# Three reorderings in a delta net: norm factors, convolutions, and the queue of four small writes

## The chip, the cores and the metric

The kernel runs on one core of a Trainium2 chip. Its time is the device time of one execution in microseconds (us); of several executions the median is given. The core's engines each work through their own list of instructions in order: TensorE (PE, matmuls), VectorE (DVE), ScalarE (ACT), GpSimd (POOL) and SyncE (SP, which here only issues DMAs). A DMA is issued by one of these engines, as an instruction in that engine's list, and then runs beside it.

## The reference

The program computes two transformer blocks for one sequence of 256 tokens with 1024 features. The change touches the first layer, a gated delta net. Cut to what matters:

```
qkv  = silu(causal_conv(hn @ w_in))        # 4 taps; q, k: 8 heads, v: 16 heads, 128 each
q, k = l2norm(q) * 128**-0.5, l2norm(k)    # the norm needs a sum over each head
m    = strict_lower((k*beta) @ k^T * decay)   # per head and chunk of 64 tokens
t    = inverse(m + I)                      # triangular solve
u, w = t @ (v*beta), t @ (k*beta*exp(gc))
... a recurrence over the chunks uses u, w, q and k
o    = rmsnorm(o) * silu(z)                # z is a fourth part of hn @ w_in
out  = o @ w_out
```

The decay comes from the gates g and beta, which are 32 more columns of `hn @ w_in`.

## The kernel before

All large products are in fp32 at higher precision: a weight chunk of 128 x 1024 is loaded by SP (`wr`, line 172), ACT copies its high part (`wh`, line 186), DVE subtracts that to give the low part (`wl`, line 187), and each product is three matmuls on PE, lines 249 to 251: high by high, high by low, low by high. Chunks have four buffers each for `wr`, `wh` and `wl`, and `_prep` asks for a chunk two chunks ahead of its use. The delta net's projections come in the order keys, gates, then a mix of q, z and v groups (`ORDER = "qqzqqzvvvvvvzvvz"`). Groups of q, k and v have matmuls of 256 columns, z groups of 512. PSUM has eight banks in one pool, `ps`.

Work that is not a projection is written as generators, "sides". `tick()` advances each side once per four weight tiles, so the point in a side's code at which it yields decides beside which projection its instructions are written. A scheduler then takes the program as written, with a priority for each instruction (its place in the program, less an offset inside `tc.high_priority`), and sets the final order on each engine from these priorities and the dependencies. `behind(i, p)` adds a dependency without a semaphore: instruction i may only stand after p in the order.

The sides and helpers that the change touches or that follow from it, all in `gdn_body`:
- `conv` (line 644): for each of two 256-column halves ACT writes tap 3 (`cy`, line 651), DVE adds taps 2, 1 and 0 (line 654), then ACT's Silu reads both halves (line 655). For q and k ACT then squares the result (`sqg`, line 665), and PE sums the squares into the bank `ssb` (line 673) after `WSSB` yields.
- `factors(0)` (line 682): when the sums of the keys are there, DVE computes the norm factors, ACT takes a logarithm (line 694), DVE adds the gates (`bgc`).
- `x_stage` (line 701): behind `factors(0)`, for each of eight head pairs PE writes `kk` = k k^T (lines 707, 708) and for two heads a bank `rp` with the gates' differences (lines 711, 712); ACT takes three exponentials of it into `EA` (lines 713 to 715), DVE multiplies `XA = -kk * EA` (line 716). After pairs 4 and 8 the diagonal 32 x 32 blocks of eight heads go to DRAM in eight small DMAs of 32 KB each (`s<-XA`, line 722). `Q[0]` is SP's queue.
- `inv_stage` (line 745): POOL reads all of that back in another layout (`NT`, line 756). DVE then does 31 steps of a substitution, each of two instructions (`fst`, line 764, and `TI`, line 766), copies the result (`TP`, line 771); SP writes `TP` and `TI` to DRAM and reads them back as blocks of `XA` and of `h`.
- `levels` (after that): 32 x 32 and 64 x 64 matmuls `y1p` (line 832), `z1p` (841, 842), `y2p` (854), `z2p` (857) for four quarters of the heads build the full inverse; between them ACT and DVE copy the results back into `Y`, `h` and `XA` (lines 833, 843, 845, 860).
- `a_stage` (line 729): PE writes `kq`, DVE multiplies it with `EA` (line 740). `evac_v` transposes v (`vtp`, line 795); `evac_z` copies z (`zt`, line 808).

Of the kernel before, what the change touches and what calls it, by code (L numbers as in the profile page):

```python
# [14 lines left out]
ALU = mybir.AluOpType  # L15
# [5 lines left out]
T = 256  # L21
# [96 lines left out]
PRIO = 0  # L118
CY = 2
CZ = 2  # L120
WSSB = 9
WVTP = 6
WINV = 10
ACCN = 4
# [18 lines left out]
class Builder:  # L143
# [31 lines left out]
    def _prep(self, j):  # L175
        if j in self.halves or j >= 2 * NCH:
            return
        nc = self.nc
        for i in range(j, j + 3):
            self._raw(i)  # L180
        r = self.raws.pop(j)
        self.raws[j] = None
        hi = self.wtile(j, F32R, "wh")
        lo = self.wtile(j, F32R, "wl")
        with self.tc.high_priority(offset=PRIO):
            nc.scalar.activation(hi, r, AF.Copy)  # L186
            i = nc.vector.tensor_tensor(lo, r, hi.bitcast(F32), ALU.subtract)  # L187
        if j in self.pins:
            self.behind(i, self.pins[j])
        self.halves[j] = (hi, lo)  # L190

    def behind(self, i, p):
# [37 lines left out]
    def w(self, name, r0, c0, width=P):  # L230
        nt = max(width // P, 1)
        self.ticks += nt
        if self.ticks >= 4:
            self.ticks -= 4
            self.tick()
        if self.n % 8 + nt > 8:
            self.n += 8 - self.n % 8
        j = self.n // 8
        for i in range(j, j + self.LA + 1):
            self._prep(i)  # L240
        self.spec.append((self.n, name, r0, c0, width))
        o = (self.n % 8) * P
        self.n += nt
        hi, lo = self.halves[j]
        return hi[:, o : o + width], lo[:, o : o + width]
# [330 lines left out]
    def gdn_body(self, gp, x):  # L576
        nc, tc, sp = self.nc, self.tc, self.sp
# [3 lines left out]
        blk = lambda b: slice(32 * b, 32 * b + 32)  # L581
# [21 lines left out]
        XA = XAb.rearrange("p k h c -> p h k c")  # L603
# [42 lines left out]
        def conv(bank, ct, dst):  # L646
            y = t2([P, 2, T], "cy")
            for i in range(2):
                u = bank[:, i * T : i * T + T]
                w = lambda j: self.col("aconv", (ct + i) * 4 + j)  # L650
                nc.scalar.activation(y[:, i], u, AF.Copy, scale=w(3))
                for j in (2, 1, 0):
                    n = 3 - j
                    nc.vector.scalar_tensor_tensor(y[:, i, n:], u[:, : T - n], w(j), y[:, i, n:], ALU.mult, ALU.add)  # L654
            nc.scalar.activation(dst, y, AF.Silu)

        kT, qT = big("kT"), big("qT")
# [2 lines left out]
        def mk_evac(dst, off, ct0, key):  # L660
            def evac(g, b):
                d = dst[:, 2 * g : 2 * g + 2]
                conv(b, ct0 + 2 * g, d)
                sq = sp.tile([P, 2, T], F32, tag="sq", bufs=2, name="sqg")
                nc.scalar.activation(sq, d, AF.Square)

                def later():
                    for _ in range(WSSB):
                        yield
                    for i in range(2):  # L670
                        for tt in range(2):
                            c = off + tt * 8 + 2 * g + i
                            nc.tensor.matmul(ssb[:, c : c + 1], sq[:, i, tt * P : tt * P + P], self.ones[:, 0:1], start=True, stop=True)  # L673
                    st[key] += 1

                self.side(later())

            return evac


        def factors(o):
            s = slice(o, o + 16)
            nc.vector.tensor_scalar(var[:, s], ssb[:, s], EPS, None, ALU.add)
            nc.vector.tensor_copy(rk[:, s], self.rsqrt(var[:, s], (P, 16)))
            if o == 0:
                nc.vector.tensor_tensor(irk[:, s], var[:, s], rk[:, s], ALU.mult)
                nc.vector.tensor_tensor(rk2[:, s], rk[:, s], rk[:, s], ALU.mult)
                for tt in range(2):
                    nc.vector.scalar_tensor_tensor(
                        lnc[:, tt * 16 : tt * 16 + 16].rearrange("p (a b) -> p a b", b=2),  # L690
                        bg[:, tt, 0:16].rearrange("p (a b) -> p a b", b=2), 1e-30,
                        rk2[:, tt * 8 : tt * 8 + 8].unsqueeze(2).to_broadcast([P, 8, 2]), ALU.max, ALU.mult)

                nc.scalar.activation(lnc, lnc, AF.Ln)
                nc.vector.tensor_tensor(bgc[:, 0:2], bg[:, 0, 32:80].rearrange("p (a b) -> p a b", b=16)[:, 0:3:2],
                                        lnc[:, 0:16].unsqueeze(1).to_broadcast([P, 2, 16]), ALU.add)
                nc.vector.tensor_tensor(bgc[:, 2], bg[:, 1, 32:48], lnc[:, 16:32], ALU.add)

        Q = [{"s": nc.sync, "a": nc.scalar, "g": nc.gpsimd}[c] for c in QS]

        def x_stage():
            while st["kss"] < 4 or not st["bg"]:
                yield
            factors(0)
            for j in range(8):
                kk = self.bank("kk")
                nc.tensor.matmul(ev3(kk)[:, 0:3:2], kT[:, j, 0:P], kT[:, j], start=True, stop=True)
                nc.tensor.matmul(kk[:, P:T], kT[:, j, P:], kT[:, j, P:], start=True, stop=True)
                for h in (2 * j, 2 * j + 1):
                    rp = self.bank("rp")  # L710
                    nc.tensor.matmul(rp[:, :384], identr[:, h : h + 1].to_broadcast([P, P]), gch, start=True, stop=False)
                    nc.tensor.matmul(rp[:, :384], identb, mask3b, start=False, stop=True)
                    nc.scalar.activation(EA[:, h, 0], rp[:, 0:128], AF.Exp, bias=bgc[:, 0, h : h + 1])
                    nc.scalar.activation(EA[:, h, 2], rp[:, 128:256], AF.Exp, bias=bgc[:, 1, h : h + 1])
                    nc.scalar.activation(EA[:, h, 1], rp[:, 256:384], AF.Exp, bias=bgc[:, 2, h : h + 1])
                    nc.vector.scalar_tensor_tensor(XA[:, h], ev3(kk), -1.0, EA[:, h], ALU.mult, ALU.mult)
                st["X"] = j + 1
                if j % 4 == 3:
                    H = slice(2 * j - 6, 2 * j + 2)
                    for b in range(4):  # L720
                        for tt in range(2):
                            Q[0].dma_start(s1[b, tt, H].rearrange("h s t -> s h t"), XA[blk(b), H, tt, blk(b)])
                if j % 4 != 3:
                    yield
                else:
                    for _ in range(4):
                        yield
# [18 lines left out]
        s1 = self.dp.tile([4, 2, 16, 32, 32], F32, name="s1")  # L746
# [38 lines left out]
        def evac_v(g, b):  # L785
            vt = t2([P, 2, T], "vt")
            conv(b, 16 + 2 * g, vt)

            def later():
                for _ in range(WVTP):  # L790
                    yield
                pt = self.bank("vtp")
                for tt in range(2):
                    for i in range(2):
                        nc.tensor.transpose(pt[:, tt * T + i * P : tt * T + i * P + P], vt[:, i, tt * P : tt * P + P], self.ident)
                for tt in range(2):
                    nc.scalar.activation(vn[:, tt, 2 * g * P : 2 * g * P + T], pt[:, tt * T : tt * T + T], AF.Copy,
                                         scale=irk[:, tt * 8 + g : tt * 8 + g + 1])
                st["v"] += 1

            self.side(later())
# [156 lines left out]
        gv = self.gemm("w_in", x, KD, list(range(16, 32)), evac_v)  # L958
        gz = self.gemm_nat("w_in", x, KD, [4096, 4608, 5120, 5632], 512, evac_z)
        self.side(x_stage())  # L960
        self.side(inv_stage())
        self.side(a_stage())
# [998 lines left out]
```

## Time and profile before

| | before |
|---|---|
| median of 3 runs | 1212.6 us (1211.88 to 1213.06) |
| the profiled execution | 1211.13 us |
| its span in the trace | 1209.3 us |
| mean granted TensorE clock | 0.997 of full speed |
| PE busy | 1185.4 us, 98% of the span |
| DVE busy | 890.1 us, 74% |
| ACT busy | 686.7 us, 57% |

The trace is of one execution. Times in it count from the start of the span. A busy share says how long an engine held an instruction, and for PE the ends of matmuls are modelled and neighbours overlap: the distance from one start to the next is what a matmul costs in a row of matmuls. In a timeline row the brackets give how long the engine stood idle before the row, and the work whose end released it.

### The profile page before, as it was taken

The page shows a single profiled execution, that of the slowest core. Times are in us where ns is not written, and L with a number is a line of the kernel's source. Part 1 is how long each engine was busy: PE and PEld are TensorE (multiplying, and loading weights), DVE is VectorE, ACT ScalarE, POOL GpSimd, SP SyncE. Part 2 cuts the span into 40 slices and gives each one's busy share as a digit, 9 for nine tenths or more (in the row PEclk, how much of TensorE's full clock was granted, in tenths as well). Part 3 has the DMA queues.
Part 4 walks back from the last instruction along what each step waited for, and adds up shares of the span by engine and source line. Part 5 has one row for each costly group of instructions (what it writes and reads, how often), then busy time and mean ns, then how long its engine had stood idle before and what let it go on. Part 6 is the DMA issues. An engine that isn't in the chain of part 4 may idle for free.

```text
span 1209.3 us, 23369 instructions
## 1 busy us (share of the span) xinstructions
PE 1185.4 (98%) x9368; PEld 1122.7 (93%) x9368; DVE 890.1 (74%) x1642; ACT 686.7 (57%) x1166; POOL 20.4 (2%) x47
## 2 busy tenths in 40 slices
PE   6999999999999999999999999999999999999997
PEld 6989988999999999989999999889799999999996
DVE  6968977668877778879977878756656567655555
ACT  4786556556655556556655556754465455444443
POOL 1000000000000001000000000000000000000000
PEclk9999999999999999999999999999999999999999
DMA  6546385454655557434655655363255563555552
GB/s 212 187 134 201 120 223 178 140 165 155 208 187 180 188 178 248 131 102 149 206 185 184 192 183 165 116 201 123 88 174 175 176 241 119 180 185 184 188 181 82
DMA packets 68205, 206.00 MB, mean 170 GB/s; under 512 B 18086, under 2 KB 18230, under 8 KB 67841
## 3 DMA queue, kind: packets, MB, share of 16 engines
q1 hardware_dynamic: 65488, 194.77, 50.3%
q0 software_dynamic: 2608, 9.75, 2.3%
q8 instruction: 73, 1.20, 0.4%
q14 instruction: 36, 0.29, 0.1%
HBM read 199.75 MB, written 4.74 MB: 169 GB/s over the span
## 4 chain that ended last, share of the span: by engine, by line
PE 92%; DVE 5%; ACT 2%; issue 1%; DMA 0%; SPq 0%; DVEq 0%; ACTq 0%
PE pb L249 21%; PE pb L250 20%; PE pb L251 20%; PE acc L249 7%; PE acc L251 7%; PE acc L250 7%; DVE wl L187 1%; PE pt L1163 1%; PE ssb L673 1%; DMA ident<-cst 0%; DVE cy L654 0%; PE kv L1567 0%; ACT wh L186 0%; PE y1p L903 0%; PE csum L366 0%
## 5 line engine op out<-in xcount | busy, mean ns | idle before, releaser
L187 DVE TENSOR_TENSOR wl<-wr,wh 128x1024 fp32r<-128x1024 f32 x362 | 442.0, 1224 | 200.0 <-ACT wh L186 198.6
L186 ACT ACTIVATE wh<-wr 128x1024 fp32r<-128x1024 f32 x362 | 381.7, 1056 | 335.8 <-issue 99.3
L249 PE MATMUL pb<-xh,wh 128*128 128x256 f32 x1224 | 347.7, 284 | 0.6 <-ACT xh L569 0.6
L251 PE MATMUL pb<-xh,wl 128*128 128x256 f32 x1224 | 345.5, 283 | 0.7 <-DVE wl L187 0.7
L250 PE MATMUL pb<-xl,wh 128*128 128x256 f32 x1224 | 345.3, 282 | 0.2 <-DVE xl L570 0.2
L249 PEld LDWEIGHTS pb<-xh,wh 128*128 128x128 f32 x1224 | 231.6, 189 | 2.7 <-issue 1.3
L250 PEld LDWEIGHTS pb<-xl,wh 128*128 128x128 f32 x1224 | 230.3, 188 | 0.5 <-DVE xl L570 0.4
L251 PEld LDWEIGHTS pb<-xh,wl 128*128 128x128 f32 x1224 | 229.5, 188 | 0.9 <-DVE wl L187 0.9
L249 PE MATMUL pb<-fh,wh 128*128 128x256 f32 x416 | 118.4, 285 | 0.0
L250 PE MATMUL pb<-fl,wh 128*128 128x256 f32 x416 | 117.5, 283 | 0.1
L251 PE MATMUL pb<-fh,wl 128*128 128x256 f32 x416 | 116.7, 281 | 0.0
L249 PE MATMUL acc<-ah,wh 128*128 128x256 f32 x352 | 98.7, 280 | 0.0
L251 PE MATMUL acc<-ah,wl 128*128 128x256 f32 x352 | 98.6, 280 | 0.0
L250 PE MATMUL acc<-al,wh 128*128 128x256 f32 x352 | 98.5, 280 | 0.0
L249 PEld LDWEIGHTS pb<-fh,wh 128*128 128x128 f32 x416 | 77.9, 188 | 1.4 <-issue 0.4
L250 PEld LDWEIGHTS pb<-fl,wh 128*128 128x128 f32 x416 | 78.2, 188 | 1.1 <-DVE fl L436 0.3
L251 PEld LDWEIGHTS pb<-fh,wl 128*128 128x128 f32 x416 | 78.9, 190 | 0.0
L1002 DVE SCALAR_TENSOR_TENSOR fy<-fpad,cols,fy 128x256 f32<-128x256 f32 x176 | 73.6, 479 | 0.0
L249 PE MATMUL pb<-wh,xh 128*128 128x512 f32 (+1 forms) x176 | 70.3, 401 | 0.0
L250 PE MATMUL pb<-wl,xh 128*128 128x512 f32 (+1 forms) x176 | 68.2, 388 | 1.1 <-DVE wl L187 1.1
L251 PE MATMUL pb<-wh,xl 128*128 128x512 f32 (+1 forms) x176 | 67.9, 386 | 0.0
L249 PEld LDWEIGHTS acc<-ah,wh 128*128 128x128 f32 x352 | 66.8, 190 | 0.0
(438 smaller groups left out, 2082.7 us busy)
## 6 DMA issues: line engine op xcount, KB each, us to landing
wr<-wall SPq DMA_DIRECT2D x362, 512.0 KB, 3.6
wzd<-zt POOLq DMA_DIRECT2D x8, 256.0 KB, 2.9
wzog<-wzd POOLq DMA_DIRECT2D x4, 512.0 KB, 4.0
bias<-bd POOLq DMA_DIRECT2D x4, 512.0 KB, 7.4
h<-xT SPq DMA_DIRECT2D x4, 256.0 KB, 4.1
h<-xT POOLq DMA_DIRECT2D x1, 1024.0 KB, 7.6
wrow<-wrow POOLq DMA_DIRECT2D x1, 1024.0 KB, 9.0
out_dram<-mw SPq DMA_DIRECT2D x4, 256.0 KB, 2.0
```

The costliest lines, as they stand in the source:

```text
L186: nc.scalar.activation(hi, r, AF.Copy)
L187: i = nc.vector.tensor_tensor(lo, r, hi.bitcast(F32), ALU.subtract)
L249: mm(out, ah, bh, start=start, stop=False, skip_group_check=skip)
L250: mm(out, ah, bl, start=False, stop=False, skip_group_check=skip)
L251: mm(out, al, bh, start=False, stop=stop, skip_group_check=skip)
L673: nc.tensor.matmul(ssb[:, c : c + 1], sq[:, i, tt * P : tt * P + P], self.ones[:, 0:1], start=True, stop=True)
L1002: nc.vector.scalar_tensor_tensor(y[:, i], u[:, i, j : j + T], w(j), y[:, i], ALU.mult, ALU.add)
L1163: nc.tensor.transpose(pt[:, j * P : j * P + P], S[:, i, j * P : j * P + P], self.ident)
```

## The change

Lines in the changed file stand 1 to 6 further down than in the file before: line 187 is the same, 249 to 251 are 250 to 252, 654 is 655, 722 is 728, 833 is 839, 843 is 849. The change has four parts.

- `WSSB` becomes a table with the value 9 for keys and for queries, as before.
- `_prep` remembers the last `wl` instruction written, and the first DVE tap of each convolution's first half may not stand ahead of it.
- `x_stage` writes `factors(0)` with a priority of 60 places earlier, and yields twice before its first head pair.
- Of the last eight small writes, the four with `tt` = 1 are issued by ACT and the other four by SP.

```diff
-WSSB = 9
+WSSB = {"kss": 9, "qss": 9}
...
         if j in self.pins:
             self.behind(i, self.pins[j])
+        self.lastwl = i
         self.halves[j] = (hi, lo)
...
                 for j in (2, 1, 0):
                     n = 3 - j
-                    nc.vector.scalar_tensor_tensor(y[:, i, n:], u[:, : T - n], w(j), y[:, i, n:], ALU.mult, ALU.add)
+                    op = nc.vector.scalar_tensor_tensor(y[:, i, n:], u[:, : T - n], w(j), y[:, i, n:], ALU.mult, ALU.add)
+                    if i == 0 and j == 2:
+                        self.behind(op, self.lastwl)
...
-                    for _ in range(WSSB):
+                    for _ in range(WSSB[key]):
...
-            factors(0)
+            with tc.high_priority(offset=60):
+                factors(0)
+            for _ in range(2):
+                yield
...
-                            Q[0].dma_start(s1[b, tt, H].rearrange("h s t -> s h t"), XA[blk(b), H, tt, blk(b)])
+                            (nc.scalar if j == 7 and tt else Q[0]).dma_start(s1[b, tt, H].rearrange("h s t -> s h t"), XA[blk(b), H, tt, blk(b)])
```

The counts of instructions stay as they were, but for the four DMA issues that go from SP to ACT. The order changes on PE from about 58 us to 217 us of the trace before, and on DVE and ACT beside it.

The first place is ACT's list around the last exponentials of `x_stage` and the first convolution of the queries behind them. The number behind `wr`, `wh` or `wl` tells one chunk's tile from another's. Before:

```order
L715 ACTIVATE EA<-rp,bgc 128x128
L651 ACTIVATE cy<-pb,cols 128x256
L186 ACTIVATE wh_1092<-wr_970 128x1024
L186 ACTIVATE wh_1139<-wr_1060 128x1024
L651 ACTIVATE cy<-pb,cols 128x256
L186 ACTIVATE wh_1163<-wr_1090 128x1024
L651 ACTIVATE cy<-pb,cols 128x256
L655 ACT_TABLE_LOAD
L655 ACTIVATE qT<-cy 128x512
```

And now:

```order
L721 ACTIVATE EA<-rp,bgc 128x128
L186 ACTIVATE wh_1136<-wr_1013 128x1024
L658 ACT_TABLE_LOAD
L658 ACTIVATE qT<-cy 128x512
L728 DMA s_208<-XA 32x8x32
L668 ACTIVATE sqg<-qT 128x512
L728 DMA s_208<-XA 32x8x32 x3
L652 ACTIVATE cy<-pb,cols 128x256
L186 ACTIVATE wh_1157<-wr_1090 128x1024
```

The four issues of line 728 stand behind a `wh` copy, the load of the activation table and the Silu of line 658, and around the Square of line 668; the convolution's `cy` of the same bank is now ahead of the exponentials.

The second place is DVE's list at the end of the inversion. Before:

```order
L766 TENSOR_TENSOR TI<-TI,fst 128x31
L654 SCALAR_TENSOR_TENSOR cy<-pb,cols,cy 128x255
L771 COPY TP<-TI 128x32x32
L654 SCALAR_TENSOR_TENSOR cy<-pb,cols,cy 128x254
L187 TENSOR_TENSOR wl_1820<-wr_1711,wh_1819 128x1024
L654 SCALAR_TENSOR_TENSOR cy<-pb,cols,cy 128x253
L187 TENSOR_TENSOR wl_1845<-wr_1747,wh_1844 128x1024
L654 SCALAR_TENSOR_TENSOR cy<-pb,cols,cy 128x255
L740 SCALAR_TENSOR_TENSOR EA<-kq,EA 128x384
```

And now:

```order
L746 SCALAR_TENSOR_TENSOR EA<-kq,EA 128x384
L655 SCALAR_TENSOR_TENSOR cy<-pb,cols,cy 128x254
L772 TENSOR_TENSOR TI<-TI,fst 128x31
L746 SCALAR_TENSOR_TENSOR EA<-kq,EA 128x384
L655 SCALAR_TENSOR_TENSOR cy<-pb,cols,cy 128x253
L777 COPY TP<-TI 128x32x32
L187 TENSOR_TENSOR wl_1845<-wr_1741,wh_1844 128x1024
L187 TENSOR_TENSOR wl_1863<-wr_1800,wh_1862 128x1024
L746 SCALAR_TENSOR_TENSOR EA<-kq,EA 128x384 x2
L187 TENSOR_TENSOR wl_1893<-wr_1842,wh_1892 128x1024
```

The taps of line 655 that stood among the weights' low parts behind `TP` now stand ahead of `TP`, and two low parts follow it at once. From the first `fst` up to `TP` there are now 37 taps (31 before) and 13 `wl` (12 before) beside the 62 steps of the inversion.

The third place is ACT's list where the levels begin. Before:

```order
L833 ACTIVATE Y_1947<-y1p 32x256
L833 ACTIVATE Y_2030<-y1p 32x256
L651 ACTIVATE cy<-pb,cols 128x256 x2
L843 ACTIVATE h<-z1p 32x2x4x32
L186 ACTIVATE wh_1972<-wr_1890 128x1024
L845 ACTIVATE XA<-z1p 32x2x4x32
L655 ACTIVATE vt<-cy 128x512
L186 ACTIVATE wh_2067<-wr_1920 128x1024
L860 ACTIVATE Y_2101<-y2p 64x512
```

And now:

```order
L186 ACTIVATE wh_1952<-wr_1890 128x1024
L839 ACTIVATE Y_1977<-y1p 32x256
L652 ACTIVATE cy<-pb,cols 128x256 x2
L849 ACTIVATE h<-z1p 32x2x4x32
L186 ACTIVATE wh_2014<-wr_1915 128x1024
L658 ACTIVATE vt<-cy 128x512
L851 ACTIVATE XA<-z1p 32x2x4x32
L839 ACTIVATE Y_2072<-y1p 32x256
L186 ACTIVATE wh_2097<-wr_1950 128x1024
L866 ACTIVATE Y_2131<-y2p 64x512
```

The copy `Y` of the second quarter (`Y_2030` before, `Y_2072` now) stood next to that of the first, and now stands behind two taps, the first quarter's copy into `h`, a `wh`, a Silu and the copy into `XA`. On PE, `y1p` of the first quarter now stands 48 matmuls of 256 columns later in the projections (384 before, 48 more now), and the stretches of about ten projection matmuls ahead of `z1p` and between `z1p` and `y2p` of the first quarter are gone.

## Rows read from the trace of the kernel before

**Rows 1.** The page: busy us (share of span) per engine; chain by engine

```profile
PE 1185.4 (98%) x9368; PEld 1122.7 (93%) x9368; DVE 890.1 (74%) x1642; ACT 686.7 (57%) x1166; POOL 20.4 (2%) x47
...
PE 92%; DVE 5%; ACT 2%; issue 1%; DMA 0%; SPq 0%; DVEq 0%; ACTq 0%
```

**Rows 2.** PE timeline, 60 to 240: start, length, work, [idle before, releaser]

```profile
72.40 0.40 PE L249 MATMUL pb<-wh,xh 128*128 128x512 f32 x1
73.80 0.44 PE L711 MATMUL rp<-gch,identr 128*128 128x384 f32 x1 [1.00 <-ACT EA L715]
...
148.61 0.50 PE L250 MATMUL pb<-wl,xh 128*128 128x512 f32 x1 [1.14 <-DVE wl L187]
...
169.79 0.21 PE L841 MATMUL z1p<-XA,Y 32*32 32x32 f32 x1 [0.46 <-ACT Y L833]
```

**Rows 3.** ACT timeline around the keys' norm factors, same columns

```profile
70.49 1.06 ACT L186 ACTIVATE wh<-wr 128x1024 fp32r<-128x1024 f32 x1 [0.91 <-PE pb L251]
71.57 1.28 ACT L713 ACT_TABLE_LOAD   x1
...
73.38 0.37 ACT L715 ACTIVATE EA<-rp,bgc 128x128 f32<-128x128 f32 x1
```

**Rows 4.** PE timeline: two neighbours of 256 columns, one of 512 between its neighbours

```profile
158.36 0.39 PE L251 MATMUL pb<-wh,xl 128*128 128x512 f32 x1
158.59 0.40 PE L249 MATMUL pb<-wh,xh 128*128 128x512 f32 x1
...
173.24 0.28 PE L250 MATMUL pb<-xl,wh 128*128 128x256 f32 x1
173.36 0.28 PE L251 MATMUL pb<-xh,wl 128*128 128x256 f32 x1
```

**Rows 5.** Second half's small writes: DVE's last product, SP's issues, ACT's Square

```profile
90.82 0.56 DVE L716 SCALAR_TENSOR_TENSOR XA<-kk,EA 128x384 f32<-128x384 f32 x1 [0.22 <-ACT EA L715]
...
91.40 5.39 SPq L722 DMA_DIRECT2D s<-XA  x8
...
99.74 0.61 ACT L665 ACTIVATE sqg<-qT 128x512 f32<-128x512 f32 x1
```

**Rows 6.** All instructions of L722: ns min/median/max, starts; landing times

```profile
L722 SPq DMA_DIRECT2D s<-XA x16: 325/449/2047, 79.8 to 96.3; - x16
...
DMA to landing us min/median/max: 1.5/2.2/3.7
```

**Rows 7.** The read of NT on POOL, and DVE's first step of the inversion

```profile
98.59 0.54 POOL L756 DMA_DIRECT2D NT<-s  x1 [17.50 <-DMA s<-XA]
...
105.62 0.19 DVE L764 TENSOR_TENSOR fst<-NT,TI 128x31 f32<-128x31 f32 x1 [1.89 <-DMA NT<-s]
```

**Rows 8.** DVE timeline behind the inversion's last step

```profile
152.89 1.08 DVE L771 COPY TP<-TI 128x1024 f32<-128x1024 f32 x1
...
155.31 0.47 DVE L654 SCALAR_TENSOR_TENSOR cy<-pb,cols,cy 128x253 f32<-128x253 f32 x1
155.71 1.21 DVE L187 TENSOR_TENSOR wl<-wr,wh 128x1024 fp32r<-128x1024 f32 x1
```

**Rows 9.** Ten microseconds: us, PE, PEld, DVE, ACT, POOL busy, clock, DMA share, GB/s

```profile
140.00:150.00 10.00, 8.86 (x66) 8.14 (x65) 10.00 (x28) 5.75 (x9) 0.00 (x0) 1.00 0.40 111
```

**Rows 10.** DMA issues, 80 to 180: KB each, median us to landing

```profile
XA<-s SPq DMA_DIRECT2D x4, 128.0 KB, 5.2
```

**Rows 11.** PE timeline at the levels

```profile
168.64 0.69 PE L832 MATMUL y1p<-h,XA 32*32 32x32 f32 x30
...
173.93 1.14 PE L854 MATMUL y2p<-h,XA 64*64 64x64 f32 x16
```

**Rows 12.** ACT timeline at the levels

```profile
170.54 0.38 ACT L833 ACTIVATE Y<-y1p 32x256 f32<-32x256 f32 x1 [0.80 <-PE y1p L832]
...
173.50 0.38 ACT L843 ACTIVATE h<-z1p 32x256 f32<-32x256 f32 x1
...
175.38 0.63 ACT L655 ACTIVATE vt<-cy 128x512 f32<-128x512 f32 x1
```


## The prediction

> **What bounds the kernel now.** I read the page first. PE is busy for 98% of the span and the chain that ended last lies on PE for 92% [rows 1], so time is won or lost only where PE idles, and the reader looks for PE's idle gaps. In the stretch whose order changes (58 to 217 us) PE's timeline shows three gaps over 0.4 us [rows 2]: 1.00 ahead of an `rp` matmul at 73.80, waiting for an exponential on ACT (it frees the bank); 1.14 at 148.61, waiting for a `wl` on DVE; and 0.46 ahead of `z1p` at 169.79, waiting for ACT's copy into `Y`. All three sum to 2.6 us, 0.21% of the time: that is the most this change can win. The second gap comes from a full DVE: from 140 to 150 it is busy for all 10.00 us, while PE is for 8.86 [rows 9]. DVE is full because the inversion's 62 steps, the convolutions' taps and the low parts share it; it is full from the inversion's first step, 105.62 [rows 7], up to about the copy `TP`, 152.89 [rows 8]. So I followed the inversion's start back: it waits for the read `NT`, which POOL issues at 98.59 after the last small write landed [rows 7], and these are SP's eight issues from 91.40 to 96.79, behind DVE's last `XA`, which ends at 91.38 [rows 5].
>
> The profiled execution took 1211.13 us with a span of 1209.3; it is 1.5 below the median of 1212.6. The sum below is a difference against that execution, and I put it on the median.
>
> **The `WSSB` table** holds the old value twice and costs nothing.
>
> **Norm factors earlier, and two yields.** In the rows, the gap at 73.80 ends with the exponential of 73.38, which ends at 73.75 [rows 2, 3]. That exponential stands behind a table load (1.28) and a `wh` of 1.06 that itself waited 0.91 for PE to free its buffer [rows 3]. ACT idled for that 0.91, so the logarithm ahead of it was done: giving the factors a higher priority does not move this chain. What moves is PE: by the order, it now has 18 instead of 16 matmuls of 512 columns ahead of that `rp`. One costs 0.23 (158.36 to 158.59, [rows 4]), so 0.5 of the 1.00 goes. Bounds: nothing, if ACT slips with PE, and 1.0. I take 0.5.
>
> The price is on the other side. The last four head pairs' `kk` now stand 24 matmuls of 256 columns later on PE. At 0.12 each (173.24 to 173.36, [rows 4]) that is 2.9 us, less the 0.5 won: the last `XA` ends at 91.4 + 2.4 = 93.8.
>
> **Four small writes on ACT.** SP's eight issues took 5.39 [rows 5], of which one took 2.05 [rows 6], so the others stand 0.48 apart; the last starts at 96.3, and POOL goes on 2.3 later. SP now has four, and is done first. ACT's four stand behind a `wh` (1.06), a table load (1.28) and a Silu (0.63) that follow the last exponential, and a Square (0.61) stands between the first and the second [rows 3, 5, 12]. The last exponential ends some 0.6 before the last `XA`, at 93.2. So: 93.2 + 1.06 + 1.28 + 0.63 = 96.2; one issue, 96.7; Square, 97.3; the last of three issues starts at 98.2. POOL goes on at 98.2 + 2.3 = 100.5, which is 1.9 later than before, and the first `fst` starts at 107.5. No row shows an issue on ACT. Bounds: if it costs ACT nothing, the last leaves at 96.8 and the inversion starts 0.5 late; if one takes 2.05 and the landing 3.7 instead of 2.2 [rows 6], 5 late. I take 1.9, from SP's usual 0.48, the nearest row. SP's next loads come up to 2 us earlier, which nothing on PE waits for here.
>
> The Trainium skill ("DMA: Bandwidth & Descriptors", section "Issuing engines are not separate DMA queues") says that DMAs started by several engines share the same 16 DMA engines, and that only the sequencer's issue time is saved. By that alone, with ACT's four free to go at once, the last of SP's four would start at 93.8 + 3 x 0.48 = 95.2 and the inversion 1.1 earlier than before: the `wl` below would come in time, and the sum would be -2.1 + 1.8 = -0.3, 1212.3, inside the second rival. The trace agrees that issue time is the larger part here, 5.39 against 2.2 for a landing [rows 5, 6].
>
> **Convolutions behind the low parts.** From the first `fst` to `TP` DVE's list now holds 37 taps instead of 31 and 13 `wl` instead of 12. A tap costs 0.40 in a full row (155.31 to 155.71) and a `wl` 1.21 [rows 8]: 6 x 0.40 + 1.21 = 3.6 us more. With the late start `TP` comes at 152.9 + 1.9 + 3.6 = 158.4. Directly behind it stands the `wl` of the last chunk of the third z block; it ends at 158.4 + 1.08 + 1.21, less 0.15 in which neighbours overlap, 160.5. Before, PE took the matmul at this place (the 39th of the block's 48) at 158.36, both gaps included; the order has nine matmuls and transposes more ahead of it, 9 x 0.12 = 1.1, so at the old pace 159.5. PE is therefore **1.0 us later** than before here: the two old gaps are replaced, not removed. Without late writes (the 0.5 bound) it would be 0.4 earlier, with 5 it would be 4.1 later; where `wl` keeps up, both gaps go and it is 2.1 earlier.
>
> **The levels.** `y1p` (168.64, [rows 11]) stands 48 matmuls later in PE's projections, 48 x 0.12 = 5.8 us. `TP` is 5.5 late and the blocks' reads (5.2 each, [rows 10]) with it, so these stay hidden. But the fillers are gone. First, `y2p` follows `z1p` of the first quarter at once and waits for ACT's copy into `h`, 0.38 [rows 12], with the hand-over 0.5; before, projections covered it. Second, a `z1p` of the second quarter then waits for its `Y`. On ACT that stands behind the copy into `h` (0.38), a `wh` (1.06), a Silu (0.63) and the copy into `XA` (as long as the first, 0.38), and takes 0.38 itself: 2.8 us. From this `y2p` covers 1.1 and the first wait 0.5, and 1.2 to 1.3 is left. Together **1.8 us**; the old 0.46 stays. Bounds: nothing, if PE runs so late that ACT's `wh` and Silu are already past, and 3, if the taps ahead of the Silu are late too.
>
> **Sum.** +1.0 at the third z block and +1.8 at the levels, +2.8 us: 1213.9 for an execution like the profiled one, 1215.4 for the median.
>
> **Rivals.**
> - *DVE keeps pace.* The low parts are now ahead of the taps, so they come in time; both gaps (1.00 as far as 2 matmuls and a free bank can cover it, and 1.14) go, and the levels find ACT free. For it: the change in order puts `wl` ahead of taps wherever the two compete, and before the late `wl` stood behind taps. Against it: DVE is full, so taps pushed back only meet the inversion. -2.1 to -2.6: 1210.0 to 1210.5. It decides if `TP` comes before 157, since then its `wl` is there at 159. This is the case on the other side: 0.13.
> - *No difference that can be told.* Runs of this kernel lie 1.2 apart, so I call 0.2%, 2.4 us, the least that can be told. The writes leave ACT without cost, the 0.5 bound: -0.4 at the z block, +1.8 at the levels, 1214.0; or my sum holds with the levels' wait halved, 1214.5. For it: writes of 32 KB can start as soon as `XA` is there. Against it: in ACT's list they stand behind 3 us of other work. 0.40.
> - *Late writes.* One of ACT's issues takes SP's 2.05 and lands in 3.7: inversion 5 late, +4.1 and +1.8, 1218.5. For it: one in sixteen did [rows 6]. Against it: ACT's list is not as full of DMAs as SP's. 0.12.
> - *My forecast*, some +2.4 to +4: 0.35.
>
> Slower by over 0.2% has 0.47, within 0.2% 0.40, faster 0.13. The likeliest case alone spans 1213.5 to 1217; with the low rivals down to 1211 and part of the late writes, 1211.0 to 1218.0.
>
> **What would show it.** In the changed profile: the gap ahead of `rp` near 73 at 0.5; the last `XA` near 93.8; four issues on ACT from 96 with the Square after the first; POOL's `NT` read near 100.5 and the first `fst` near 107.5; `TP` near 158.4; a PE gap that ends with the `wl` behind `TP` near 160.5; PE gaps of 0.5 and 1.3 at `y2p` and the second quarter's `z1p`. I am wrong if POOL's read starts at or before 98.6, if `TP` comes before 157, or if PE's gaps at the levels stay at 0.5 in all.

## The result, and the profile after

The changed kernel took 1222.36 us (median of 6 runs, five of them from 1220.33 to 1223.72), the kernel before 1212.24 in 6 runs beside it: a ratio of 1.0081 (95% interval 1.0070 to 1.0092), **some 10 us slower**. The sixth run took 1441.81 us at a mean granted clock of 0.75 and stays out of the ratio. I had forecast 2.8 us slower, and a range from 1211.0 to 1218.0.

The profiled execution of the changed kernel has a span of 1220.4 us. Its page (busy us and share by engine; the granted clock in tenths, in 40 slices) answers to [rows 1]:

```profile
PE 1193.9 (98%) x9368; PEld 1128.7 (92%) x9368; DVE 887.8 (73%) x1642; ACT 686.6 (56%) x1166; POOL 20.2 (2%) x47
...
PEclk9999998999999999999999999999999999999999
```

PE is busy for 8.5 us longer than before with as many matmuls, and one slice, the seventh (183 to 214 us), has no 9 in the clock. So PE did not only wait more, it also ran slower. The gaps first. PE's timeline (start, length, work, [idle before, releaser]) has these six over 0.4 us in the stretch, against three of 1.00, 1.14 and 0.46 in [rows 2]:

```profile
74.86 0.45 PE L717 MATMUL rp<-gch,identr 128*128 128x384 f32 x1 [0.54 <-ACT EA L721]
...
112.61 0.61 PE L676 MATMUL ssb<-ones,sqg 128*128 128x1 f32 x4 [1.19 <-ACT sqg L668]
...
146.68 0.55 PE L801 MATMUL vtp<-ident,vt 128*128 128x128 f32 x3 [1.31 <-ACT vt L658]
...
178.49 0.21 PE L847 MATMUL z1p<-XA,Y 32*32 32x32 f32 x1 [0.46 <-ACT Y L839]
...
181.45 1.97 PE L860 MATMUL y2p<-h,XA 64*64 64x64 f32 x16 [1.80 <-ACT h L849]
184.10 0.31 PE L847 MATMUL z1p<-XA,Y 32*32 32x32 f32 x2 [0.68 <-ACT Y L839]
```

They sum to 5.98 us, 3.4 more than before. The gap at `rp` has shrunk to 0.54, as forecast. The one at a `wl` is gone, and so is the one that was forecast in its place, behind `TP`; but two new ones of 1.19 and 1.31 wait for ACT's Square and Silu, and the levels have three, 0.46, 1.80 and 0.68, where before there was one. Within the gap of 1.80 the clock falls. Stretches of 2 us of the changed kernel (PE, PEld, DVE, ACT, POOL busy; granted clock; DMA share; GB/s):

```profile
180.00:182.00 2.00, 0.55 (x5) 0.55 (x6) 1.41 (x3) 1.43 (x3) 0.00 (x0) 0.65 0.04 8
182.00:184.00 2.00, 1.42 (x14) 1.23 (x12) 1.96 (x4) 1.81 (x4) 0.00 (x0) 0.50 0.00 0
184.00:186.00 2.00, 1.90 (x39) 1.40 (x41) 1.27 (x2) 1.93 (x4) 0.00 (x0) 0.50 0.44 147
...
190.00:192.00 2.00, 2.00 (x54) 1.64 (x55) 1.77 (x5) 0.34 (x1) 0.00 (x0) 0.79 0.40 113
```

From 180.6 to 190.8 us the granted clock is 0.50, that is 1.2 of 2.4 GHz, and it had been 1.00 in [rows 9]. The mean of 0.65 in the first stretch (1.00 ahead of the fall, 0.50 behind it) puts the fall 0.6 behind its start: inside the gap that ends at 181.45, and ahead of the gap of 0.68, which therefore has no part in it. A matmul of 512 columns is 0.24 behind its neighbour ahead of the levels (163.58) and 0.43 within this stretch (187.94):

```profile
163.58 0.40 PE L251 MATMUL pb<-wl,xh 128*128 128x512 f32 x1
163.82 0.40 PE L252 MATMUL pb<-wh,xl 128*128 128x512 f32 x1
...
187.94 0.63 PE L250 MATMUL pb<-wh,xh 128*128 128x512 f32 x1
188.37 0.63 PE L251 MATMUL pb<-wl,xh 128*128 128x512 f32 x1
```

From one matmul ahead of the stretch whose order changed (38.33 us before, 39.38 after) to the same one well behind it (421.34 and 432.15) it takes 383.0 us before and 392.8 after, **9.8 more**. Idle gaps make 3.0 us of this before and 6.9 after; the other 5.9 are longer distances between matmuls. Of the 11.1 us between the two profiled executions 1.05 lies ahead of 27 us, where both programs are the same; it belongs to the execution and not to the change.

The chain that I followed reads so after, to be laid beside [rows 5], [rows 7] and [rows 8]; these times include the 1.05. ACT's issues and the table load among them:

```profile
95.11 0.37 ACTq L728 DMA_DIRECT2D s<-XA  x1
95.37 1.28 ACT L658 ACT_TABLE_LOAD   x1
...
97.34 1.33 ACTq L728 DMA_DIRECT2D s<-XA  x3
```

POOL's read, and on DVE the last `XA`, the first `fst` with what is queued behind it, `TP` and the `wl` behind it:

```profile
102.62 0.54 POOL L762 DMA_DIRECT2D NT<-s  x1 [20.11 <-DMA s<-XA]
```

```profile
94.53 0.55 DVE L722 SCALAR_TENSOR_TENSOR XA<-kk,EA 128x384 f32<-128x384 f32 x1
...
109.44 0.19 DVE L770 TENSOR_TENSOR fst<-NT,TI 128x31 f32<-128x31 f32 x1 [4.03 <-DMA NT<-s]
109.55 1.22 DVE L187 TENSOR_TENSOR wl<-wr,wh 128x1024 fp32r<-128x1024 f32 x1
110.69 0.47 DVE L655 SCALAR_TENSOR_TENSOR cy<-pb,cols,cy 128x253 f32<-128x253 f32 x1
...
160.13 1.08 DVE L777 COPY TP<-TI 128x1024 f32<-128x1024 f32 x1
161.05 1.20 DVE L187 TENSOR_TENSOR wl<-wr,wh 128x1024 fp32r<-128x1024 f32 x1
```

The first issue on ACT leaves at 95.11, ahead of the table load and the Silu behind which it stands in ACT's list; the other three leave beside the Square (97.33 to 97.96) and not behind it. So an issue did not wait here for the end of the work ahead of it. `NT` is read at 102.62 (98.59 before), the first `fst` starts at 109.44 (105.62), `TP` at 160.13 (152.89). DVE stands idle for 4.03 ahead of `fst`, with a `wl` and a convolution's last tap queued behind it; that tap is ready only at 111.16, and with it the Silu and the Square for which PE waits at 112.61.

### The profile page after: what moved, and what is told of

Its sections match the earlier page's. It is cut to its first block, busy times and chain, and to the rows that moved or that the text cites. A ratio compares the mean times of both kernels' runs of the same rounds, so it can differ in the third digit from the quotient of the medians.

```text
span 1220.4 us, 23374 instructions
## 1 busy us (share of the span) xinstructions
PE 1193.9 (98%) x9368; PEld 1128.7 (92%) x9368; DVE 887.8 (73%) x1642; ACT 686.6 (56%) x1166; POOL 20.2 (2%) x47
## 4 chain that ended last, share of the span: by engine, by line
PE 90%; DVE 4%; ACT 3%; DMA 1%; issue 1%; SPq 0%; ACTq 0%; DVEq 0%; POOLq 0%
PE pb L250 20%; PE pb L251 20%; PE pb L252 20%; PE acc L250 7%; PE acc L251 7%; PE acc L252 7%; DVE wl L187 1%; DVE cy L655 1%; DMA NT<-s 1%; PE pt L1169 1%; PE ssb L676 0%; DMA ident<-cst 0%; ACT wh L186 0%; PE kv L1573 0%; PE y1p L909 0%
```

## The experiments

All stand beside runs of the kernel before on the same chip; the ratio is to these.

**Which part makes it slow.** First the changed kernel with the writes back on SP:

```diff
-(nc.scalar if j == 7 and tt else Q[0]).dma_start(
+Q[0].dma_start(
```

> The changed kernel with all eight last small writes issued by SP again; norm factors, yields and the order of the taps as changed. Theory of the two yields (they put the head pairs, the inversion's start and the levels later against the projections, so DVE stands blocked behind the first fst, the first levels have no projections beside them, and TensorE's clock then falls to half): the read NT still starts near 102 to 103, PE still idles over 2 us around y2p, the clock still falls to 0.5 there, 1220 to 1224 us. Theory of the writes (ACT's four, issued late and landing in up to 4.2 us, make the inversion late and all else follows): NT starts near 99 to 100, the first fst by 107, no clock at 0.5 near 181, 1211 to 1215 us.

1219.19 us, ratio 1.0054 (1.0033 to 1.0075). POOL's read comes 1.7 earlier than in the changed kernel (0.45 of it is the start of the execution), and the gap ahead of `y2p` is the same:

```profile
100.96 0.54 POOL L762 DMA_DIRECT2D NT<-s  x1 [18.89 <-DMA s<-XA]
```

```profile
179.12 1.44 PE L860 MATMUL y2p<-h,XA 64*64 64x64 f32 x16 [1.80 <-ACT h L849]
```

The gap of 1.19 at `ssb` is gone, the clock is at 0.50 from 180 to 190. So by the medians the writes on ACT cost some 3 us in this company, and two thirds of the loss is something else. The 3 us are loose: the intervals of the two ratios overlap, and between the two profiled executions the stretch from 39 to 432 us differs by 1.2. Neither theory had it: NT came 1 us earlier than the yields' said, the time stayed 4 above the writes'.

The changed kernel without the yields:

```diff
             with tc.high_priority(offset=60):
                 factors(0)
-            for _ in range(2):
-                yield
```

> The changed kernel without the two yields behind the norm factors; the early factors, the taps behind the low parts and the four writes on ACT stay. Theory of the yields: PE's order is nearly that of the kernel before again, with projections beside the first levels; last XA near 91.5, NT read at 98 to 101, no half clock, 1210.5 to 1214 us. Theory of the writes: NT read at 101 or later, DVE blocked behind fst, 1217 us or more. A third, that the taps' new place costs the time: DVE's gaps against PE stay, 1216 or more with NT at 99.

1220.46 us, ratio 1.0061 (1.0041 to 1.0081): against the theory that it is all the yields. `NT` is read at 94.76, earlier than in the kernel before, and still the time is lost. The loss sits in another place. On ACT the copy `Y` of `y2p` (line 864 there) stands behind a `wh` and a Silu, and these wait for PE and for taps:

```profile
182.69 1.06 ACT L186 ACTIVATE wh<-wr 128x1024 fp32r<-128x1024 f32 x1 [1.94 <-PE pb L251]
184.55 0.63 ACT L658 ACTIVATE vt<-cy 128x512 f32<-128x512 f32 x1 [0.80 <-DVE cy L655]
185.19 0.59 ACT L864 ACTIVATE Y<-y2p 64x512 f32<-64x512 f32 x1
```

PE idles for 3.12 us ahead of `z2p`, and the clock is at 0.50 from 186 to 192. To tell which part does this, the yields alone and the taps alone, each in the kernel before:

```diff
             factors(0)
+            for _ in range(2):
+                yield
```

> The kernel before with the two yields alone (factors, taps and writes as before). Theory of the yields: the same shape as the changed kernel, half clock near the first levels, 1219 to 1224 us. Theory of the writes, or of the taps: 1210 to 1215 us.

1219.20 us, ratio 1.0047 (1.0030 to 1.0064). The gaps at the levels are 0.46, 1.80 and 1.35 and the clock falls, though `NT` is read at 99.51, only 0.9 later than before (`TP`, at 156.67, is 3.8 later). So the gap at `y2p` needs no late writes. The gap of 1.31 at `vtp` is there too.

```diff
-nc.vector.scalar_tensor_tensor(y[:, i, n:], u[:, : T - n], w(j), ...)
+op = nc.vector.scalar_tensor_tensor(y[:, i, n:], u[:, : T - n], w(j), ...)
+if i == 0 and j == 2:
+    self.behind(op, self.lastwl)
```

> The kernel before with the first tap of each convolution held behind the last low part, and nothing else. Theory that this order alone makes the other long gap (in the run without the yields ACT's copy Y of y2p stood behind a Silu that waited for taps on DVE, and PE idled 3.1 ahead of z2p): a gap of 2.5 to 3.5 ahead of z2p, the clock at 0.5 behind it, 1218 to 1221.5 us. Theory that it takes ACT's writes or the early factors beside it: no such gap, 1211 to 1215 us.

1218.92 us, ratio 1.0059 (1.0037 to 1.0081). The gap ahead of `z2p` is there to the hundredth, and within it the clock falls:

```profile
183.83 1.43 PE L860 MATMUL z2p<-XA,Y 64*64 64x64 f32 x11 [3.12 <-ACT Y L863]
```

The gap at the `wl` near 147, which holding back the taps might have removed, stays at 1.13. The same with v's taps left free (`and ct < 16` in the condition):

> The kernel before with the taps held behind the last low part for the queries and keys alone, not for v. By the theory that v's taps, pushed back, make the Silu of vt late, and ACT's copy Y behind it, and so PE's gap of 3.1 ahead of z2p: no gap there, no fall of the clock, 1211 to 1214 us. If the taps of the queries and keys do it through the start of the inversion: 1217 us or more.

1211.87 us, ratio 1.0003 (0.9987 to 1.0018), no gap at `z2p`, no fall at the levels. It is v's taps; the way through the Silu of `vt` and the copy behind it is read from ACT's rows, the same with the taps alone (the Silu waits 0.81 for taps) as without the yields (0.80).

**The parts that cost little.** The writes on ACT alone:

> The kernel before with four of the last eight small writes issued by ACT and nothing else. Theory of the yields: the writes cost or win at most 1.5 us, 1211 to 1214.5. Theory of the writes: the inversion is 2 us or more late, 1217 or more. If a second queue saves issue time alone: NT is read 1 to 2 us earlier than at 98.6.

1214.34 us, ratio 1.0016 (1.0001 to 1.0031). In this order ACT issues the four at once, and POOL reads `NT` 3.3 us earlier than in [rows 7]:

```profile
91.12 1.89 ACTq L723 DMA_DIRECT2D s<-XA  x4
...
95.32 0.54 POOL L757 DMA_DIRECT2D NT<-s  x1 [14.52 <-DMA s<-XA]
```

Of this, 0.3 is the start of the execution. The rest is issue time: 1.89 for four against 5.39 for eight [rows 5], 3.5 saved. The rule quoted from the Trainium skill ("DMA: Bandwidth & Descriptors", section "Issuing engines are not separate DMA queues"), that a second issuing engine saves only this, agrees with the trace. It buys nothing here: `TP` comes at 153.04, since DVE is full in between, and the time is if anything longer. The factors alone, and both together:

```diff
-            factors(0)
+            with tc.high_priority(offset=60):
+                factors(0)
```

> The kernel before with the norm factors at the higher priority and nothing else. The gap of 1.00 ahead of rp should shrink by half or more if sums of the queries' squares now stand behind it; all else as before: 1210.5 to 1213 us. By my prediction (the factors' priority moves nothing in that chain): the gap stays at 1.0, 1211.5 to 1213.5.

> The kernel before with the higher priority and the four writes on ACT, without yields and without the taps' new place. If gaps add up: what the two do alone, together 1211.5 to 1214.5, with the read NT near 95.3 as with the writes alone, and no fall of the clock. If the pieces work on each other through the order: 1216 or more, with a gap at the levels.

1211.46 us, ratio 0.9990 (0.9979 to 1.0000), and 1213.65, ratio 1.0016 (1.0002 to 1.0029). With the factors alone the gap at `rp` is gone. ACT's chain there is as it was (table load, `wh`, table load, exponentials); six sums of the queries' squares now stand on PE ahead of that `rp` and cover the wait. That is 0.5 to 1 us, at the edge of what can be told. With both together `NT` is read at 97.09, of which 2.1 is a late start, and there is no gap beyond the usual 0.46 at the levels. But in its profiled execution, at 1217.96 the slowest of ten, PE idles for 1.40 and 0.71 ahead of transposes at 217 and 218 (`otp`), and the clock is at 0.50 from 219 to 222.6: "no fall of the clock" did not hold there.

**Is the fall of the clock a cost of its own?** The changed kernel with matmuls of ones put into the gaps at the levels, in banks that the real matmuls then overwrite:

```diff
+by = self.bank("y2p") if qy is not None else None
+if qy is not None and qz is None:
+    for _ in range(12):
+        nc.tensor.matmul(by[:, 0:128], self.ones, self.ones, start=True, stop=True)
...
+bz = self.bank("z1p")
+if q == 1:
+    for _ in range(4):
+        nc.tensor.matmul(bz[:, 0:128], self.ones, self.ones, start=True, stop=True)
```

> The changed kernel with sixteen added matmuls of ones by ones (128 x 128) on PE, which write banks that the real matmuls then overwrite: twelve in the bank of the first quarter's y2p, four in that of the second quarter's z1p, where PE idled 0.46, 1.80 and 0.68. They need nothing, so they can run in the idle time; the copies on ACT that PE waits for come no earlier. If the fall of the clock after the gaps is a cost of its own: the granted clock stays at 1.0 from 178 to 192, y2p still starts near 181.5, and the time is 1216 to 1218.5. If only the waits cost time, or the clock falls for another reason: 1221 to 1225 us, clock 0.5 as before.

1220.53 us, ratio 1.0064 (1.0049 to 1.0079). The clock holds:

```profile
180.00:182.00 2.00, 2.00 (x40) 1.84 (x30) 1.75 (x5) 1.79 (x4) 0.00 (x0) 1.00 0.00 0
182.00:184.00 2.00, 2.00 (x25) 1.93 (x24) 1.58 (x3) 1.95 (x4) 0.00 (x0) 1.00 0.00 0
184.00:186.00 2.00, 2.00 (x84) 1.56 (x84) 1.23 (x1) 1.33 (x4) 0.00 (x0) 1.00 0.82 258
```

So, in the executions profiled, PE's idling at the levels is what makes the clock fall. The time lies between the two answers, since the added matmuls cost more than the idle time they fill. How much more, the trace shows from the first `y1p` to the second quarter's first `z1p`, 7.64 here and 6.76 in the changed kernel (177.34 to 184.10), so 0.9 of added work does not fit:

```profile
176.49 0.69 PE L838 MATMUL y1p<-h,XA 32*32 32x32 f32 x30
...
181.97 1.14 PE L868 MATMUL y2p<-h,XA 64*64 64x64 f32 x16
...
184.13 0.22 PE L838 MATMUL y1p<-h,XA 32*32 32x32 f32 x2
```

From there to the same matmul 26.8 us on in the changed kernel it took 23.9 here. **The clock's price is these 2.9 us**; less the 0.9 that leaves 2.0, and the medians lie 1.8 apart, though the two intervals just overlap. The `y2p` ahead of that `z1p` is 1.97 long at half clock and 1.14 at full, but this costs nothing: `z1p` waits for ACT's `Y` and comes 2.65 behind the start of `y2p` in the changed kernel, 2.64 without the writes and 2.65 with the yields alone, where `y2p` takes 1.97, 1.44 and 1.29.

With fewer, seven and five:

> The changed kernel with added matmuls of ones by ones again, now twelve: seven in the bank of y2p, of which five come to stand ahead of z1p's rest and two behind it, and five asked for in that of the second quarter's z1p (four ahead of it by the order). In the first try PE was still busy with them when ACT's copies were there: 1.3 us beyond at y2p and 0.9 at z1p. With these the real y2p should start about 4.2 us behind y1p and z1p of the second quarter about 6.7, as in the changed kernel (4.1 and 6.8). If the fall of the clock costs 5 us of its own: clock 1.0 throughout, 1216.5 to 1218.5. If it costs nothing beside the gaps: 1220.5 or more.

1221.24 us, ratio 1.0080 (1.0065 to 1.0095), which by its bounds says that the clock costs nothing. I don't read it so. At the levels the clock held again, and the same stretch took 24.3, 2.5 less. But in the profiled execution it fell at another place, to 0.50 at 114 to 117, behind a gap of 1.64 at `ssb`, which is 1.66 in the run with sixteen, where it did not fall; from 38 us up to the first `y1p` this execution lost 2.0 us against the changed kernel's. Whether the other three executions fell there too is not recorded. By its median this run is inconclusive on the price.

**Why the copy into `h` is late.** In the changed kernel ACT's row at 180.53 shows a `cy` waiting for taps, and `h` behind it:

```profile
178.47 0.47 ACT L652 ACTIVATE cy<-pb,cols 128x256 f32<-128x256 f32 x1
180.53 0.47 ACT L652 ACTIVATE cy<-pb,cols 128x256 f32<-128x256 f32 x1 [1.59 <-DVE cy L655]
181.02 0.37 ACT L849 ACTIVATE h<-z1p 32x256 f32<-32x256 f32 x1
181.42 1.06 ACT L186 ACTIVATE wh<-wr 128x1024 fp32r<-128x1024 f32 x1
182.64 0.63 ACT L658 ACTIVATE vt<-cy 128x512 f32<-128x512 f32 x1 [0.17 <-DVE cy L655]
183.28 0.37 ACT L851 ACTIVATE XA<-z1p 32x256 f32<-32x256 f32 x1
183.67 0.37 ACT L839 ACTIVATE Y<-y1p 32x256 f32<-32x256 f32 x1
```

I wrote tap 3 of both halves first, so that the second `cy` waits for no taps:

```diff
+for i in range(2):
+    nc.scalar.activation(y[:, i], bank[:, i * T : i * T + T], AF.Copy, scale=w3(i))
 for i in range(2):
-    nc.scalar.activation(y[:, i], u, AF.Copy, scale=w(3))
     for j in (2, 1, 0):
```

> The changed kernel, but each convolution writes tap 3 of both halves on ACT first, and DVE then adds the taps of both. ACT's second cy then waits for no taps, and the copy into h behind it comes as soon as z1p is done. If the 1.8 us gap ahead of y2p is this wait (1.6 us by the rows): gap under 0.7 there, and no fall of the clock, or a shorter one; 1213 to 1218 us. If the copy into h is late for another reason: the gap stays over 1.5 and the clock falls, 1220 or more.

1222.89 us, ratio 1.0092 (1.0076 to 1.0107). The gap at `y2p` is down to 0.47, so that wait was its cause. But it came back one step on, longer:

```profile
180.78 1.14 PE L861 MATMUL y2p<-h,XA 64*64 64x64 f32 x16 [0.47 <-ACT h L850]
185.44 0.31 PE L848 MATMUL z1p<-XA,Y 32*32 32x32 f32 x2 [3.52 <-ACT Y L840]
```

```profile
183.02 0.63 ACT L659 ACTIVATE vt<-cy 128x512 f32<-128x512 f32 x1 [2.30 <-DVE cy L656]
...
184.62 0.38 ACT L852 ACTIVATE XA<-z1p 32x256 f32<-32x256 f32 x1
185.01 0.38 ACT L840 ACTIVATE Y<-y1p 32x256 f32<-32x256 f32 x1
```

Now the Silu waits 2.30 for all six taps, and the copies into `XA` and `Y` stand behind it; within PE's gap the clock falls to 0.50, from 183.3 to 193.6. The kernel before with the same edit, with and without the factors, and the factors with ACT's copies at a higher priority:

> The kernel before with tap 3 of both halves first and nothing else. There projections covered the same wait of ACT, so by my theory little is to be won: 1209.5 to 1213 us. If the wait cost something elsewhere (the gap of 1.14 at wl comes from a full DVE, which this does not relieve): under 1209.5.

> The kernel before with the higher priority of the factors and tap 3 of both halves first, a try at a kernel better than both. The gap at rp goes, 0.5 to 1.0 us: 1209 to 1212 us. If pieces work on each other through the order: 1213 or more.

> A try at a better kernel: the kernel before with the factors at the higher priority, and ACT's copies at the levels (Y, h and XA) at a priority of 300 places earlier, which puts the copy Y of y2p ahead of a wh copy and XA ahead of a Silu. The gap at rp goes (0.5 us by the run with the factors alone), the gap of 0.46 at z1p stays: 1210 to 1212 us. If a wh pushed back makes the projections wait: 1213 or more.

1213.39 (ratio 1.0014, 1.0005 to 1.0023), 1211.74 (0.9996, 0.9987 to 1.0005) and 1212.16 (1.0004, 0.9995 to 1.0014). None beats the kernel before by what can be told; the best is the factors alone, at 0.9990.

## Why the prediction was wrong

The direction was right and the size was not: 10 us and not 2.8. Two steps failed: the wait of `y2p`, priced at one copy, and the premise that time is lost "only where PE idles". By its steps:

- *`rp` and the last `XA`.* The gap of 0.54 is the 0.5 forecast. The last `XA` ends at 95.1; less the 1.05 of the start that is 94.0, with 93.8 forecast.
- *Writes on ACT.* The last issue at 98.2 is the number forecast, but by luck: the first issue and the Square, which the sum put in line, did not delay the others, so the last left 3.1 behind the last `XA` and not 4.4, and the late start made up for it. The landing was mis-sized: POOL went on 4.4 after the last issue, not 2.3 (ACT's last two writes took 4.2 and 3.9 to land, where [rows 6] has 3.7 as the longest). Less the start, `NT` is read 3.0 later than before, with 1.9 forecast. Late writes also cost through a step that I did not have: `fst` waits at the head of DVE's list and holds up a tap and a `wl`, and PE idles 1.19 at `ssb`. I read DVE's idle time ahead of `fst` [rows 7] as slack, and did not ask who waits for what is queued behind it.
- *Taps and low parts up to `TP`.* 3.6 forecast; from `fst` to `TP` it takes 50.7 now and 47.3 before, 3.4. The `wl` behind `TP` ends at 162.3, with 160.5 forecast. PE takes the matmul there at 162.31 (158.36 before): 2.9 later less the start, with 2.1 forecast. But PE does not idle there for 0.15 or more; the gaps at `ssb` and `vtp`, which no term had, had made it late in part.
- *The levels.* Forecast 0.5 at `y2p` and 1.3 at the second quarter's `z1p`; measured 1.80 and 0.68 (the second would be 1.5 at full clock, since `y2p` took 0.83 longer). The step that failed is that `y2p` waits for ACT's copy into `h` alone, 0.38, and with the hand-over 0.5. Behind ACT's first `cy` of the pair stands a second that waits for three taps, and the copy is behind both. The trace of before shows the very same wait:

```profile
173.00 0.47 ACT L651 ACTIVATE cy<-pb,cols 128x256 f32<-128x256 f32 x1 [1.58 <-DVE cy L654]
```

  There, projections on PE covered it. I named these fillers as gone and then priced only the copy, not what stood ahead of it in ACT's list. The run with both halves first shows it: gap 0.47 without that wait.
- *The clock.* No term had it; "time is won or lost only where PE idles" left no room for matmuls that run at half pace. It is about 3 of the 10 us, and all three kernels in which PE idled 1.8 or more at the levels beside short gaps, and the three with 3.1 or 3.5 ahead of one matmul, show a fall there. The trace before had it too, elsewhere. In an attention stage PE idles for 0.92 and 1.97 in short succession, and the clock, 1.00 until 532, has a mean of 0.66 from 532 to 536:

```profile
530.46 0.43 PE L1156 MATMUL ob<-ptS,vn 128*64 128x256 f32 x1 [0.92 <-DVE ptS L1166]
...
533.51 0.80 PE L249 MATMUL acc<-oh,wh 128*128 128x256 f32 x2 [1.97 <-ACT oh L432]
```

```profile
528.00:532.00 4.00, 2.62 (x21) 1.55 (x19) 3.54 (x8) 4.00 (x15) 0.00 (x0) 1.00 0.60 169
532.00:536.00 4.00, 2.49 (x11) 2.50 (x12) 2.90 (x11) 1.94 (x8) 0.00 (x0) 0.66 0.62 224
```

  I had searched for gaps only in the stretch that the change touches, and never looked at what a gap of this length does afterwards.

Of the rivals, "late writes" gave 1218.5 by a wrong path. That v's taps alone cost 6 us was in none of them, and the trace of the changed kernel could not show it: with the yields beside them it has no gap at `z2p`. The parts do not add up: yields 7, taps 6 and writes 2 alone, but 10 together.

Open: of the 9.8 us in the stretch 3.9 are idle gaps, 0.8 is the longer `y2p` (it stands where PE would else have waited) and 2.9 are the half clock behind it, together 7.6. The other 2.2 lie in distances between matmuls, which I can't assign to a part. Why the gap at `ssb` is 1.19 in one kernel and 1.66 in another with the same code there is open too.

## What to carry to other kernels

When a change takes independent work away from beside a chain that crosses engines, price the whole queue ahead of each hand-over, waits included: what was hidden is in the trace as a wait that cost nothing. A first instruction that waits for a DMA holds up all that is queued behind it on its engine. And a gap on PE can cost more than its length (1.80 us of it went with 2.9 at half clock here), so look in the trace for what the granted clock did at gaps of that length before pricing a new one.

## What the runs showed of the hardware

At an idle time of 1.80 among small matmuls the clock fell to 0.50 for 10 us: in the changed kernel within it, with all writes on SP and with the yields alone 0.7 and 0.9 behind its end. Within one of 3.12 it fell for 10 us in one run (the taps alone) and for 7 in another (without the yields). The length alone did not decide: behind an idle time of 1.64 the clock fell for some 3 us, and behind one of 1.66 at the same place in another kernel it did not; behind 1.40 and 0.71 it fell for some 3 us (factors and writes), and behind 1.48 and 0.71 at the same place it did not (factors alone).

At the start the listed clock is no reading. Between 18 and 20 us both executions list 1.00, yet the one has 19 matmuls and the other 11. Stretches of the kernel before and of the changed kernel, with the counts behind PE's busy time:

```profile
18.00:20.00 2.00, 2.00 (x19) 2.00 (x19) 2.00 (x5) 0.68 (x2) 0.00 (x0) 1.00 0.36 98
```

```profile
18.00:20.00 2.00, 2.00 (x11) 2.00 (x10) 2.00 (x5) 0.39 (x2) 0.00 (x0) 1.00 0.35 98
```

The trace's first clock record stands at 14.49 us before and at 20.16 in the changed kernel; ahead of it the view lists 1.00 without a record. In the changed kernel the distance between two matmuls of 256 columns goes from 0.21 (19.58 to 19.79) to 0.12 (20.20 to 20.32) just there. Most of what this execution lost by 20 us stays: at 27 us it is the 1.05 us by which it runs late.
